# Five heads' queries and keys by seven block products, with the attention of all eight heads placed behind them

## The chip, the core and the metric

The program runs on one core of one Trainium2 chip. A core has five engines that each work through an instruction stream of their own in order: PE (TensorE, the matrix multiplies), DVE (VectorE), ACT (ScalarE), POOL (GpSimd) and SP (SyncE, which here only issues DMA transfers). They meet at semaphores. The metric is device time in microseconds of one execution, as the median of several runs; lower is better.

## The reference

One streaming step of an encoder layer: 512 prompt frames and 64 sample frames, 576 in all, each 2048 wide. What matters here is the first half of the layer, the projection and the attention:

```
hn = rmsnorm(x, g_norm1)
proj = hn @ w_in                      # 2048 x 6144: q, k, v, gb, gc, hc, 1024 columns each
q = rmsnorm(q.reshape(B, T, 8, 128), g_q);  k = rmsnorm(k.reshape(B, T, 8, 128), g_k)
z = q k^T / sqrt(128)                 # per head; mask: key before query
log_1mb = where(mask, log_sigmoid(-z), 0)
after = reverse_cumsum(log_1mb) - log_1mb
w = where(mask, exp(log_sigmoid(z) + after), 0);  o_attn = w @ v
```

The prompt attends to itself, the sample frames attend to 512 cached frames and themselves. A gated convolution over the other columns, an output projection, and a SwiGLU feed-forward layer (2048 to 5632 and back) follow; new keys and values are outputs too. Everything is float32.

## The kernel before

Activations lie feature-major: a tile is 128 features by 576 frames, cut into two halves of 288 (`HALVES`). A float32 product is made of three passes of a reduced float32 type: each operand is split into a high part and the rest (`split`: ACT copies the high part, DVE subtracts it), and PE adds high x high, low x high, high x low. One column block of 128 outputs of `w_in` takes 16 row blocks x 3 passes x 2 halves = 96 matmuls of 128x288.

**Order of work.** PE's order is written by hand, as the program records it. Side work runs as generators in a small pipeline: `pipe.tick()` is called after every three matmuls of a column (a **tick**), and `yield n` puts the rest of a generator n ticks later. SP's order is by hand too behind head 0. DVE, ACT and POOL are ordered by a scheduler, which works before the run with its own idea of how long things take. Their streams are then fixed: an instruction that waits holds all that stand behind it on its engine.

**Heads.** `head(h)` projects three column blocks, q, k and v of one head: 96 ticks. `norm_evac` normalises q and k (per frame, over 128 features): a transpose out of PSUM, squares, sums, one small matmul on PE (`ss`, L664), an inverse square root on 128x18 numbers, a scaling of 128x576, a transpose back, the gain, a split into `qh, ql` or `kh, kl`. `attend(h)` then does, each step some ticks behind the last: the scores (L730, L733) of four key blocks into three PSUM banks `z0` to `z2`; the scores of sample frames `zs`; softplus and splits of the three banks (ACT, DVE, POOL); the reverse sums as triangular matmuls (three carry groups, L780 to L783, L786 to L789, L792 to L795), after each of which `weights` caps the diagonal block (L771), takes the exponential and splits it; the product with the values `po` (L801, L804), for which `vh, vl`, the split values, are made; and `cz` and `os` for the sample frames. Between the last carry group and `po` stand 16 ticks, between `po` and `cz` 18, between `cz` and `os` 16.

**Sums of x.** The convolution columns already use block products (Strassen's scheme in Winograd's form): a unit of two column blocks by two halves of frames takes seven products of eight row blocks (24 matmuls each) and not eight. For it `conv_prepare` makes the sums of weights (DVE), their split (`whl`: ACT and DVE), and four sums of x, which `x_sums` makes during the heads: 8 pairs, 66 ticks each, through DRAM.

## Time and profile before

| | us |
|---|---|
| three runs | 2346.26, 2345.19, 2344.64 (median 2345.19) |
| profiled execution, span from first to last instruction | 2344.4 (no other time of it is given) |
| PE busy in that span | 2332.3 |
| DVE busy | 1872.3 |
| ACT busy | 1142.2 |
| POOL busy | 256.6 |

The span less the busy time of PE is 12.1 us. The granted TensorE clock is 1.000 throughout. The eight heads lie between about 32 and 435 us of the span; a period of one head is 47.2 us. A busy PE counts a matmul from its start to its modelled end (295 ns for 128x288); two that follow each other start closer than that, and the distance from start to start is what a matmul costs.

### The profile page before, as it was taken

The numbers are of one execution on the slowest core, as the hardware profiler recorded it, in microseconds if no ns is written. First come the engines' busy times: TensorE is split into PE (matmuls) and PEld (weight loads), VectorE is DVE, ScalarE is ACT, GpSimd is POOL, SyncE is SP. The second block draws the span as 40 slices with busy tenths as digits, with TensorE's granted clock in tenths as the row PEclk, the third lists the DMA queues.
The fourth block names the chain that finished last, engine by engine and source line by source line (L and its number), as shares of the span: only waits on it lengthen the run. The fifth ranks groups of instructions, "written<-read, shape, count | busy, mean of one in ns | idle before, by whom it ended". The sixth has DMA issues, their size and how long they took to land.

```text
span 2344.4 us, 43718 instructions
## 1 busy us (share of the span) xinstructions
PE 2332.3 (99%) x17573; PEld 2325.2 (99%) x17573; DVE 1872.3 (80%) x2827; ACT 1142.2 (49%) x1994; POOL 256.6 (11%) x362
## 2 busy tenths in 40 slices
PE   8999999999999999999999999999999999999999
PEld 8999999999999999999999999999999999999999
DVE  7766665788877889888888888888888777987886
ACT  6655555444445555444444444444444444444444
POOL 1111111111111220000000000000000001431121
PEclk9999999999999999999999999999999999999999
DMA  8665563774378555345345354344444936885653
GB/s 269 157 173 142 138 167 105 253 232 129 111 244 229 177 172 168 123 151 157 112 155 157 115 158 151 121 154 138 139 154 133 357 119 207 222 240 188 201 135 100
DMA packets 581762, 395.74 MB, mean 169 GB/s; under 512 B 90686, under 2 KB 570680, under 8 KB 581560
## 3 DMA queue, kind: packets, MB, share of 16 engines
q1 hardware_dynamic: 572072, 376.24, 51.7%
q0 software_dynamic: 8624, 16.22, 3.4%
q8 instruction: 137, 2.24, 0.4%
q10 hardware_dynamic: 864, 0.49, 0.1%
q14 instruction: 65, 0.53, 0.1%
HBM read 301.46 MB, written 91.44 MB: 168 GB/s over the span
## 4 chain that ended last, share of the span: by engine, by line
PE 97%; DVE 2%; DMA 1%; ACT 1%; issue 0%; SPq 0%; ACTq 0%
PE psy L1604 35%; PE psw L1604 18%; PE pj L221 15%; PE psx L1604 9%; PE psy L1094 6%; PE pjo L221 4%; PE psw L1094 3%; PE psx L1094 1%; PE pjz L221 1%; PE z L733 1%; PE po L804 1%; PE os L834 0%; PE zs L759 0%; DMA raw_a<-in_w_in_dram 0%; DMA xin<-in_x_prompt_dram 0%; DVE whl L1066 0%
## 5 line engine op out<-in xcount | busy, mean ns | idle before, releaser
L1604 PE MATMUL psy<-h_s,whl 128*128 128x288 f32 x2787 | 411.0, 294 | 0.0
L221 PE MATMUL pj<-x,whi 128*128 128x288 f32 x1856 | 388.1, 297 | 0.3 <-DVE x L375 0.3
L1604 PEld LDWEIGHTS psy<-h_s,whl 128*128 128x128 f32 x2787 | 383.3, 188 | 0.0
L231 DVE TENSOR_TENSOR whl<-raw_a,whl 128x1024 fp32r<-128x1024 f32 (+4 forms) x296 | 321.2, 1086 | 57.8 <-ACT whl L230 56.7
L1604 PE MATMUL psw<-t,whl 128*128 128x288 f32 x2400 | 347.6, 294 | 0.0
L1604 PEld LDWEIGHTS psw<-t,whl 128*128 128x128 f32 x2400 | 327.3, 188 | 0.3 <-DVE whl L231 0.2
L230 ACT CAST whl<-raw_a 128x1024 fp32r<-128x1024 f32 (+4 forms) x296 | 268.3, 907 | 101.7 <-issue 35.4
L221 PEld LDWEIGHTS pj<-x,whi 128*128 128x128 f32 x1856 | 303.5, 189 | 1.0 <-DVE x L375 0.6
L221 PE MATMUL pj<-x,wlo 128*128 128x288 f32 x928 | 274.2, 295 | 0.1
L231 DVE TENSOR_TENSOR whl<-raw_b,whl 128x1024 fp32r<-128x1024 f32 (+5 forms) x190 | 197.6, 1040 | 65.5 <-ACT whl L230 64.3
L230 ACT CAST whl<-raw_b 128x1024 fp32r<-128x1024 f32 (+5 forms) x190 | 165.4, 872 | 165.4 <-issue 72.7
L1614 ACT COPY part<-psy 128x288 f32<-128x288 f32 x242 | 96.4, 398 | 284.9 <-PE psy L1604 283.7
L1604 PE MATMUL psy<-b22m,whl 128*128 128x288 f32 x1212 | 183.1, 295 | 0.0
L1604 PE MATMUL psy<-t2t,whl 128*128 128x288 f32 x1212 | 182.8, 294 | 0.0
L221 PEld LDWEIGHTS pj<-x,wlo 128*128 128x128 f32 x928 | 174.6, 188 | 0.7 <-DVE wlo L442 0.3
L1604 PE MATMUL psx<-h_s,whl 128*128 128x288 f32 x1185 | 173.2, 294 | 0.0
L1604 PEld LDWEIGHTS psy<-t2t,whl 128*128 128x128 f32 x1212 | 168.1, 188 | 0.2 <-DVE whl L231 0.2
L1604 PEld LDWEIGHTS psy<-b22m,whl 128*128 128x128 f32 x1212 | 167.9, 188 | 0.0
L1604 PEld LDWEIGHTS psx<-h_s,whl 128*128 128x128 f32 x1185 | 162.5, 188 | 0.0
L230 ACT CAST whl<-s 128x1024 fp32r<-128x1024 f32 (+5 forms) x81 | 72.3, 892 | 101.9 <-PE psw L1604 101.9
L1383 POOL DMA_DIRECT2D hid_dram<-form x3 | 2.2, 750 | 971.1 <-DVE form L231 971.1
L1604 PE MATMUL psy<-t,whl 128*128 128x288 f32 x576 | 106.7, 295 | 0.0
(483 smaller groups left out, 4246.2 us busy)
## 6 DMA issues: line engine op xcount, KB each, us to landing
hid_dram<-form SPq DMA_DIRECT2D x147, 288.0 KB, 3.0
raw_a<-in_w_in_dram SPq DMA_DIRECT2D x41, 1024.0 KB, 6.3
raw_a<-in_w_gate_dram SPq DMA_DIRECT2D x22, 1024.0 KB, 5.8
raw_a<-in_w_up_dram SPq DMA_DIRECT2D x22, 1024.0 KB, 5.9
raw_b<-in_w_gate_dram SPq DMA_DIRECT2D x22, 1024.0 KB, 7.4
raw_b<-in_w_up_dram SPq DMA_DIRECT2D x22, 1024.0 KB, 6.6
h_s<-hid_dram SPq DMA_DIRECT2D x10, 2016.0 KB, 11.8
raw_a<-in_w_out_dram SPq DMA_DIRECT2D x16, 1024.0 KB, 5.7
```

The source lines that it names most:

```text
L221: mm(ps, w_[:, k, csl], x_, start=(k == 0 and n == 0), stop=(k == nk - 1 and n == 2))
L230: nc.scalar.copy(out=hi, in_=src)
L231: (lo_eng or nc.vector).tensor_tensor(out=lo, in0=src, in1=hi.bitcast(F32), op=ALU.subtract)
L733: mm(zb[i], a_[:, kk], b_[:, q0:TP], start=(n == 0), stop=False, skip_group_check=True)
L804: mm(po[:, i * P : 512], a_[:, i, :], b_[:, : 512 - i * P], stop=(i == 0 and n == 2), **kw)
L1094: mm(ps, whl[:, w_, j, :], x_, start=(start and j == 0 and q == 0), stop=(j == m - 1 and q == 2), skip_group_check=True)
L1383: q.dma_start(out=hid_dram[fp][2 * n - 2 : 2 * n].rearrange("f p t -> p f t"), in_=t.bitcast(F32))
L1604: mm(ps, whl[:, w_, j, :], x_, start=(start and j == 0 and q == 0), stop=(j == len(xs_) - 1 and q == 2), skip_group_check=True)
L1614: nc.scalar.copy(out=t, in_=st["y"])
```

## The change

Of the 16 blocks of queries and keys, those of heads 2 to 6 are now made by units of seven block products (`unit_prepare`, `unit_run`): columns q and k of a head by two halves of the frames, 35 products of 24 matmuls. Heads 0 and 1 (`EARLY`) come first as plain columns, in whose time `x_sums` makes the four sums of x for all 8 pairs, 12 ticks a pair, into SBUF (`xf`, `first_form`); they go to DRAM later for the convolution (`store_sums`). Then the 35 products; then, as plain columns, all values and head 7 (`LATE`, ten columns of 32 ticks). Queries and keys no longer go from PSUM into the normalisation: they are stored raw to DRAM (`put_raw`) and loaded again by `attend`, which now holds the normalisation too. `attend(h)` starts at tick 4 + 42 h of `LATE`; heads stood 96 ticks apart before. Its steps are closer: last carry group to `po` 10 ticks, `po` to `cz` 11, `cz` to `os` 11; and with heads 42 ticks apart and 101 ticks long, the normalisation of head h+1 (`ss` of q and of k) falls between the carry groups and `po` of head h. The values are loaded from DRAM shortly before `po`. Weights of `LATE` have one buffer in place of two (the other half is scratch). Counted over the whole program, PE has 120 matmuls of 128x288 fewer (16812 for 16932); ACT has 46 instructions more, DVE 36 more, SP 45 DMA issues more. Pairs of work tiles (`hl`) move to a pool of their own.

```diff
+UNIT_HEADS = (2, 3, 4, 5, 6)
+EARLY = [(0, 0), (1, 0), (0, 1), (1, 1)]
+LATE = [(2, 0), (2, 1), (2, 2), (2, 3), (2, 4), (0, 7), (1, 7), (2, 5), (2, 6), (2, 7)]
+PERIOD = 42
...
+    qk_dram = tc.dram_tile([2 * NH, P, T], F32, name="qk_dram")
...
+    for j, h in EARLY + LATE:
+        col_chunk(w_in, j * AW + h * P)
...
+    def split_later(i, end):
+        yield 8
+        if i + 1 < end:
+            split_weight(nc.vector)
+        yield 6
+        if i >= len(EARLY) and i + 2 < end:
+            load_weight()
...
+            if i == first_out - 2:
+                split_weight(nc.vector)
+            else:
+                pipe.spawn(split_later(i, end))
...
+    def load_pair_x(j, a, b):
+        x_pair[j] = [a, b]
+        for r in range(2):
+            if b is not last_x or r == 0:
+                nc.sync.dma_start(out=x_pair[j][r], in_=xt_dram[2 * j + r])
...
+            ev, od = x_pair[j]
             ge, go = g1c[:, 2 * j : 2 * j + 1], g1c[:, 2 * j + 1 : 2 * j + 2]
-            nc.scalar.activation(out=b11, in_=b11, func=AF.Copy, scale=ge)
-            nc.scalar.activation(out=b22, in_=b22, func=AF.Copy, scale=go)
-            yield 8
-            stt(out=b11, in0=b12, scalar=ge, in1=b11, op0=ALU.mult, op1=ALU.subtract)
-            yield 8
-            stt(out=b12, in0=b12, scalar=ge, in1=b22, op0=ALU.mult, op1=ALU.subtract)
-            yield 8
-            put(four[:, 0:2, :], (0, 2))
-            yield 8
-            tt(out=b22, in0=b22, in1=b11, op=ALU.subtract)
-            yield 8
-            stt(out=b21, in0=b21, scalar=go, in1=b22, op0=ALU.mult, op1=ALU.subtract)
-            yield 8
-            put(four[:, 2:4, :], (3, 1))
-            yield 8
-        free_places.append(True)
...
+            ta, tb, tc_, td = (tmp.tile([P, HALF], F32, tag=tag, name=f"x{tag}{j}") for tag in ("sq", "r", "sq", "r"))
+            nc.scalar.activation(out=ta, in_=ev[:, :HALF], func=AF.Copy, scale=ge)
+            nc.scalar.activation(out=tb, in_=od[:, HALF:], func=AF.Copy, scale=go)
+            yield 3
+            stt(out=ta, in0=ev[:, HALF:], scalar=ge, in1=ta, op0=ALU.mult, op1=ALU.subtract)
+            stt(out=tc_, in0=ev[:, HALF:], scalar=ge, in1=tb, op0=ALU.mult, op1=ALU.subtract)
+            yield 3
+            tt(out=tb, in0=tb, in1=ta, op=ALU.subtract)
+            stt(out=td, in0=od[:, :HALF], scalar=go, in1=tb, op0=ALU.mult, op1=ALU.subtract)
+            yield 2
+            split(xf[2][:, j, 0, :], xf[2][:, j, 1, :], tc_)
+            first_form[j] = slot(PLACE[j], f"xf0_{j}", F32R).rearrange("p (f t) -> p f t", f=2)
+            split(first_form[j][:, 0, :], first_form[j][:, 1, :], ta)
+            yield 2
+            split(xf[1][:, j, 0, :], xf[1][:, j, 1, :], tb)
+            split(xf[3][:, j, 0, :], xf[3][:, j, 1, :], td)
+            if j == 0:
+                load_pair_x(5, last_place(1), last_place(2))
+                load_pair_x(7, last_place(3), last_x)
+            if j in (1, 3):
+                load_pair_x(3 + j, slot(2 * j - 1, f"x{j}a"), slot(2 * j + 1, f"x{j}b"))
...
+        yield 16
+        turn("q")
+        yield 2
+        turn("k")
+        yield 4
+        qf, qh, ql = norm("q", gqs, TP)
+        yield 3
+        kb = t1.tile([P, T], F32, tag="kb", name="kb")
+        kf, kh, kl = norm("k", col("gk"), 3 * P, kb)
+        yield 2
+        nc.vector.transpose(out=cK, in_=cK)
+        yield 12
...
+        yield 3
+        put_tokens(kb, kp[:, h, :], 0, TP)
+        put_tokens(kb, ks[:, h, :], TP, T)
+        yield 14
+        vtok = t1.tile([P, 5, P], F32, tag="vtok", name="vtok")
+        nc.sync.dma_start(out=vtok[:, 0:4, :], in_=vt_dram[h, :TP].rearrange("(i p) d -> p i d", p=P))
+        nc.sync.dma_start(out=vtok[:, 4, :], in_=vt_dram[h, T - P :])
         yield 2
-        yield 8
-        kb = st["kb"]
-        if h:
-            put_tokens(kb, kp[:, h, :], 0, TP)
-            put_tokens(kb, ks[:, h, :], TP, T)
+        cV = t1.tile([P, 4, P], F32, tag="cV", name="cV")
+        nc.sync.dma_start(out=cV, in_=cv[:, h, :].rearrange("(i p) d -> p i d", p=P))
...
-        yield 18
...
         weights(2)
-        yield 5
+        yield 3
...
         weights(1)
-        yield 5
+        yield 3
...
         weights(0)
-        yield 16
-        vtok, vh, vl = st["vtok"], st["vh"], st["vl"]
+        yield 1
+        sp = scratch[:, 1280 : 1280 + T]
+        softplus(sp[:, :320], zc, sp[:, :320])
+        nc.gpsimd.tensor_tensor(out=sp[:, 256:320], in0=sp[:, 256:320], in1=s01, op=ALU.mult)
+        sh = t1.tile([P, T], F32R, tag="sph", name="sph")
+        sl = t1.tile([P, T], F32R, tag="spl", name="spl")
+        rest = sp[:, 320:]
+        nc.gpsimd.tensor_copy(rest[:, 192:256], sp[:, 256:320])
+        for b in (2, 1, 0):
+            nc.gpsimd.tensor_tensor(out=rest[:, b * TS : (b + 1) * TS], in0=rest[:, (b + 1) * TS : (b + 2) * TS],
+                                    in1=sp[:, (b + 1) * TS : (b + 2) * TS], op=ALU.add)
+        split(sh, sl, sp)
+        nc.sync.dma_start(out=vp[:, h, :].rearrange("(i p) d -> p i d", p=P), in_=vtok[:, 0:4, :])
+        nc.sync.dma_start(out=vs[:, h, :], in_=vtok[TS:, 4, :])
+        vh = t1.tile([P, 3, P], F32R, tag="vh", name="vh")
+        vl = t1.tile([P, 3, P], F32R, tag="vl", name="vl")
+        split(vh, vl, vtok[:, 0:3, :])
+        yield 9
         po = misc("po")
-        assert h < 6 or free_places
...
+        yield 11
         cz = misc("cz")
...
-        yield 16
+        yield 11
...
+    hwanted = [(0, 0, 0), (0, 0, 1), (1, 0, 0), (0, 1, 0), (0, 1, 1), (1, 0, 1), (1, 1, 0), (1, 1, 1)]
+    hwanted += [(n, c, s) for n in range(2, NHU) for c in range(2) for s in range(2)]
...
+        if first_sum:
+            tt(out=raw(1, 0), in0=raw(1, 0), in1=raw(0, 0), op=ALU.subtract)
+            if p_ == 6:
+                tt(out=own, in0=raw(1, 0), in1=raw(1, 1), op=ALU.add)
+        src = own if p_ in (3, 6) else raw(*{1: (0, 0), 2: (0, 1), 4: (1, 1), 5: (1, 0), 7: (1, 0)}[p_])
+        bt["turn"] = bt.get("turn", 0) + 1
+        whl = hoper[n, p_] = wpool.tile([P, 2, NP, P], F32R, tag=("whi", "wlo")[bt["turn"] % 2], name="whl")
+        nc.scalar.copy(out=whl[:, 0], in_=src)
+        if first_sum and p_ == 7:
+            tt(out=own, in0=raw(1, 0), in1=raw(1, 1), op=ALU.add)
+        tt(out=whl[:, 1], in0=src, in1=whl[:, 0].bitcast(F32), op=ALU.subtract)
+        gone.append(p_)
...
+        def multiply(ps, start):
+            whl = hoper.pop((n, p_))
+            for j in range(NP):
+                if p_ in (5, 6, 7, 4):
+                    q = {5: 0, 6: 1, 7: 2, 4: 3}[p_]
+                    t = xf[q][:, j] if q else first_form[j]
+                    xh, xl = t[:, 0, :], t[:, 1, :]
+                else:
+                    xh, xl = x_two(2 * j + (p_ > 1), int(p_ == 3))
+                for q, (w_, x_) in enumerate(((0, xh), (1, xh), (0, xl))):
+                    mm(ps, whl[:, w_, j, :], x_, start=(start and j == 0 and q == 0), stop=(j == NP - 1 and q == 2),
+                       skip_group_check=True)
+                pipe.tick()
...
+    def put_raw(i, ps, a, b, part=None):
+        t = tmp.tile([P, HALF], F32, tag="y", name="raw")
+        if part is None:
+            nc.scalar.copy(out=t, in_=ps)
+        else:
+            nc.vector.tensor_tensor(out=t, in0=ps, in1=part, op=ALU.add)
+        nc.sync.dma_start(out=qk_dram[i][:, a:b], in_=t)
...
+    horder = [(0, 1), (0, 2), (1, 1), (0, 7), (0, 6), (0, 5), (0, 3), (0, 4), (1, 2), (1, 6), (1, 7), (1, 5)]
+    for n in range(2, NHU):
+        if n < NHU - 1:
+            horder += [(n, 1), (n - 1, 3), (n - 1, 4), (n, 2), (n, 6), (n, 7), (n, 5)]
+        else:
+            horder += [(n, 1), (n - 1, 3), (n - 1, 4), (n, 6), (n, 7), (n, 5), (n, 2), (n, 4), (n, 3)]
...
+    def first_units():
+        yield 15
+        bt["own"] = dpool.tile([P, UC], F32, tag="uc", name="own")[:, :1024].rearrange("p (j c) -> p j c", c=P)
+        call_blocks(range(5))
...
+    for i, (j, h) in enumerate(EARLY[1:]):
+        if i == len(EARLY) - 2:
+            pipe.spawn(first_units())
+        project(raw_evac(j, h), (None, "z1") if i == 0 else (None, None))
+    for q in (2, 3):
+        unit_prepare(*horder[q])
+    pipe.flush()
+    pipe.spawn(store_sums())
+    for k_, (n, p_) in enumerate(horder):
+        unit_run(n, p_)
+        if k_ + 4 < len(horder):
+            unit_prepare(*horder[k_ + 4])
...
+        pipe.spawn(attend(h), 4 + PERIOD * h)
+    for j, h in LATE:
+        project(values_evac(h) if j == 2 else raw_evac(j, h))```

How the change stands in the streams, at three places. Names: `z_n` is a PSUM bank with scores of one head, `Eq, Ek` the queries and keys frame-major, `qf, kf` the same feature-major, `t, y, r, ms` the small numbers of the inverse square root, `whl` a split block operand, `xr` and `xf` sums of x.

**First place: DVE between the last carry group of a head and its `po`.** Before (head 4), from the cap of the second bank on:

```order
L771 SCALAR_TENSOR_TENSOR z_3130<-z_3130,acA 128x128
L178 TENSOR_TENSOR wlo_3365<-raw_a,whi_3364 128x1024
L688 TENSOR_REDUCE sums<-sq 128x9
L178 TENSOR_TENSOR wlo_3365<-raw_a,whi_3364 128x1024
L231 TENSOR_TENSOR vl<-vtok,vh 128x384
L231 TENSOR_TENSOR pl_3139<-pr_3133,ph_3136 128x384
L771 SCALAR_TENSOR_TENSOR z_3129<-z_3129,acA 128x128
L231 TENSOR_TENSOR pl_3138<-pr_3132,ph_3135 128x512
```

Now (head 1); three rows ahead of this piece stands `L823 ... z_2790`, the cap of the last bank, and the piece is the normalisation of head 2 up to its `kl`, and behind it `vl` of head 1:

```order
L738 SCALAR_TENSOR_TENSOR ms<-ss,rpad_t 128x18
L744 TENSOR_TENSOR Eq<-Eq,r 128x576
L751 STREAM_TRANSPOSE qf<-Eq 128x576
L245 TENSOR_TENSOR pl_2799<-pr_2793,ph_2796 128x512
L741 SCALAR_TENSOR_TENSOR t<-y 128x18
L742 TENSOR_TENSOR t<-t,ms 128x18
L743 SCALAR_TENSOR_TENSOR r<-t,y 128x18
L744 TENSOR_TENSOR Ek<-Ek,r 128x576
L245 TENSOR_TENSOR ql<-qf,qh 128x512
L751 STREAM_TRANSPOSE kf<-Ek 128x576
L245 TENSOR_TENSOR kl<-kf,kh 128x384
L245 TENSOR_TENSOR vl<-vtok,vh 128x384
```

The same piece of ACT's stream (head 1 with the normalisation of head 2):

```order
L244 CAST ph_2796<-pr_2793 128x512
L740 ACTIVATE y<-y 128x18
L752 ACTIVATE qf<-qf,gqs 128x576
L244 CAST qh<-qf 128x512
L752 ACTIVATE kf<-kf,vec 128x576
L244 CAST kh<-kf 128x384
L244 CAST vh<-vtok 128x384
L869 COPY o_oa<-po 128x512
```

`vl` stood beside the cap of the last bank in every head; now it stands behind the keys of the next head. On DVE there are 16, 13, 17, 4, 12, 16 and 14 instructions between the two for heads 0 to 6 (for head 7, which has no next head, none). For heads 2 and 5 they hold two evacuations and the transpose of values (`Ev`) too, for head 6 a transpose of `Ev` and one other 128x576 operation, for heads 0, 2 and 6 half a weight split (`wlo`) and for head 3 both halves, ahead of the normalisation. In head 4 `vl` stands before the transpose of the keys.

**Second place: DVE where the first products begin.** The last rows of `x_sums`, and the first operands of the units:

```order
L669 SCALAR_TENSOR_TENSOR xr_1068<-st_504,g1c,xr_1066 128x288
L245 TENSOR_TENSOR xf_585<-xr_1066,xf_585 128x288
L245 TENSOR_TENSOR xf_587<-xr_1068,xf_587 128x288
L927 TENSOR_TENSOR whl<-raw_a,whl 128x1024 x2
L918 TENSOR_TENSOR raw_a<-raw_a 128x1024
```

All 64 DVE instructions of `x_sums` stand ahead of the first `whl`. On SP the five loads of raw weights for the units stand behind the store of the third early column's second half (`L1001 DMA qk_dram<-raw`), whose copy out of PSUM stands on ACT among the copies of `x_sums` for pair 6.

**Third place: ACT where `LATE` begins.**

```order
L181 CAST whi_2163<-raw_a 128x1024 x2
L998 COPY raw<-psy 128x288
L181 CAST whi_2282<-raw_a 128x1024 x2
L728 ACTIVATE raw_a<-Eq 128x576
L728 ACTIVATE raw_a<-Ek 128x576
L739 ACTIVATE y<-ms 128x18
```

The squares of head 0 (`L728`) stand behind the split of the second late column's weights (`whi_2282`), whose load is issued when the first one's split is done.

More of the change, by code (lines that the diff above doesn't have):

```diff
@@ L452, in tile_hybrid_stream_step @@
             square(*squares.pop(0))
-        nc.sync.dma_start(out=xt_dram[KD - 1], in_=stores[0][1])
+        last_x = stores[0][1]
+        nc.sync.dma_start(out=xt_dram[KD - 1], in_=last_x)
         turn_vectors()
@@ L619, in x_sums @@
     def x_sums():
-        raw = o_half[1][:, 2:4, :]
-        four = raw.rearrange("p k (i t) -> p (k i) t", i=2)
-        b11, b12, b21, b22 = (four[:, q, :] for q in range(4))
         stt, tt = nc.vector.scalar_tensor_tensor, nc.vector.tensor_tensor
-        def put(two, names):
-            split(xs_out[:, :, 0, :], xs_out[:, :, 1, :], two)
-            for r, q in enumerate(names):
-                nc.sync.dma_start(out=xs_dram[q, j].rearrange("f p t -> p f t"), in_=xs_out[:, r].bitcast(F32))
+        yield 3
@@ L725, in attend @@
+        pl = [t1.tile([P, (512, 384, 256)[i]], F32R, tag=f"pl{i}", name=f"pl{i}") for i in range(3)]
         full = (512, 384, 384)
@@ new lines, in unit_prepare, with raw @@
+    def unit_prepare(n, p_):
+        st, tt = hst.setdefault(n, {"gone": []}), nc.vector.tensor_tensor
+        gone, own = st["gone"], bt["own"]
+        first_sum = p_ in (6, 7) and 6 not in gone and 7 not in gone
+        def raw(c, s):
+            return hregion[n, c, s][1]
+        if first_sum:
[10 more added lines that the diff above has]
+        gone.append(p_)
+        if p_ in (6, 7) and not first_sum:
+            tt(out=raw(1, 0), in0=own, in1=raw(0, 0), op=ALU.add)
+            tt(out=own, in0=raw(0, 1), in1=own, op=ALU.subtract)
+        free = {4: [(1, 1)], 5: [(1, 0)]}.get(p_, [])
+        if p_ in (2, 6, 7) and all(q in gone for q in (2, 6, 7)):
+            free = [(0, 0), (0, 1)]
+        call_blocks([hregion.pop((n, c, s))[0] for c, s in free])
@@ L978, in evac_gb @@
         def evac_gb(ps, a, b):
-            if not bt:
+            if "pool" not in bt:
                 open_b()
```

366 lines of the change are left out of this document (202 added, 164 removed).

## Prediction

> **What bounds the kernel now.** I read the page first, its busy times and the shares of the chain that ended last, then the waits of PE.
>
> ```profile
> span 2344.4 us, 43718 instructions
> PE 2332.3 (99%) x17573; PEld 2325.2 (99%) x17573; DVE 1872.3 (80%) x2827; ACT 1142.2 (49%) x1994; POOL 256.6 (11%) x362
> PE 97%; DVE 2%; DMA 1%; ACT 1%; issue 0%; SPq 0%; ACTq 0%
> ```
> ```profile
> PE psx_s L352 <- POOL acA L268: 5.0, 1, 5.0
> PE psy L1094 <- DVE whl L1066: 0.7, 1, 0.7
> ```
>
> PE is the bound from end to end. Its longest wait, 5.0 us, is at the start; nowhere else does it wait for as long as a microsecond. So a matmul that goes away is worth its whole distance to the next one, and a wait put into PE's stream costs its whole length. Next, the windows of a stage with heads and of the present block products:
>
> ```profile
> 200.00:250.00 50.00, 50.00 (x373) 49.50 (x372) 34.90 (x66) 29.63 (x59) 7.86 (x15) 1.00 0.63 177
> 550.00:600.00 50.00, 50.00 (x380) 50.00 (x379) 40.33 (x50) 21.50 (x29) 8.34 (x14) 1.00 0.38 112
> ```
>
> The columns are the window's length, then PE, PEld, DVE, ACT and POOL with counts, clock, DMA share and GB/s. Among the heads DVE has 15 us in 50 to spare and ACT 20. Block products leave DVE 10 in 50, and PE is full all the same.
>
> **What is removed: 120 matmuls.** The chain of waits gives their distance and the period of a head:
>
> ```profile
> 251.22 11.15 PE pj L221 x84
> 298.42 11.15 PE pj L221 x84
> 227.89 0.22 PE po L801 x2
> 228.11 1.58 PE po L804 x9
> 240.99 0.13 PE ss L664 x2
> ```
>
> 84 matmuls of 128x288 in 11.15 us are 0.1327 us each, so 120 are **-15.9 us**. A head's period is 298.42 - 251.22 = 47.2 us; its 288 column matmuls take 38.2, so its attention has 9.0 us of PE, which the change keeps.
>
> **What the products add.** 35 operands, each an ACT copy and a DVE subtraction of 128x1024, four sums of weights per head, evacuations, 32 stores and 16 loads of raw rows. The present products do the same per unit beside the same 168 matmuls (22.3 us), and the second window shows PE full with DVE at 40 of 50: nothing on the path. Without that cover a unit would cost DVE's 40/50 of 22.3, 18 us.
>
> **Where the products begin.** All sums of x are made in the time of three columns. Prices from the groups of instructions, the present x_sums (lines 639 to 647):
>
> ```profile
> L639 DVE SCALAR_TENSOR_TENSOR o_ob<-o_ob,g1c 128x288 f32<-128x288 f32 x8 | 5.1, 639 | 3.1 <-ACT o_ob L636 3.1
> L647 DVE SCALAR_TENSOR_TENSOR o_ob<-o_ob,g1c 128x288 f32<-128x288 f32 x8 | 4.7, 583 | 0.1
> L641 DVE SCALAR_TENSOR_TENSOR o_ob<-o_ob,g1c 128x288 f32<-128x288 f32 x8 | 4.1, 515 | 0.9 <-ACT o_ob L637 0.5
> L645 DVE TENSOR_TENSOR o_ob<-o_ob 128x288 f32<-128x288 f32 x8 | 3.6, 450 | 0.1
> L231 DVE TENSOR_TENSOR hf<-acc_a,hf 128x288 fp32r<-128x288 f32 x2 | 0.9, 458 | 2.2 <-ACT hf L230 1.9 <-DMA raw_a<-in_w_in_dram 0.2
> L178 DVE TENSOR_TENSOR wlo<-raw_a,whi 128x1024 fp32r<-128x1024 f32 x51 | 61.8, 1216 | 8.3 <-ACT whi L177 8.3
> ```
>
> Now DVE's timeline, where it is never idle:
>
> ```profile
> 267.39 1.22 DVE L178 TENSOR_TENSOR wlo<-raw_a,whi 128x1024 fp32r<-128x1024 f32 x1
> 268.52 0.55 DVE L231 TENSOR_TENSOR vl<-vtok,vh 128x384 fp32r<-128x384 f32 x1
> 268.99 0.55 DVE L231 TENSOR_TENSOR pl<-pr,ph 128x384 fp32r<-128x384 f32 x1
> ```
>
> From start to start it is 1.13 and 0.47: instructions that don't need each other overlap by 0.08 us. A pair of x costs 0.64 + 0.58 + 0.52 + 0.45 + 4 x 0.46 - 8 x 0.08 = 3.4 us, eight pairs 27; with a weight split (2.3) and two copies (0.9) some 30 us. DVE can start these near 42.5 us of the span and is done at about 73; the first product is due on PE near 71.7 us (three columns of 12.7 from 32, and 1.6 of small matmuls), and its operand takes another 1.1. I take **+2**; bounds 0 (a later due time) and 5 (the raw weights are called only after an ACT copy that stands among the sums).
>
> **Where LATE begins.** The load of the second column's weights is issued when the first products' end frees the path on SP, and head 0's squares stand behind their split.
>
> ```profile
> raw_a<-in_w_in_dram SPq DMA_DIRECT2D x41, 1024.0 KB, 6.3
> o_ob<-xt_dram SPq DMA_DIRECT2D x8, 576.0 KB, 7.0
> ```
>
> Issued at 1.3 us, landed near 8 (weights and Eq alike, 6.3 and 7.0); two ACT copies and two subtractions later, near 12, the sums of q are ready, which PE wants at tick 26, 10.4 us: 2 us. The keys, one transpose, one square and one reduction behind, cost 1 more; then the split of the third column's weights stands among the chain to the first scores: 3. I take **+6**; bounds 0 and 9.
>
> **The wait at po: the large term.** The timeline of one key normalisation, DVE and then ACT:
>
> ```profile
> 288.35 0.18 DVE L668 SCALAR_TENSOR_TENSOR ms<-ss,rpad_t 128x18 f32<-128x18 f32 x1
> 289.49 0.18 DVE L673 SCALAR_TENSOR_TENSOR r<-t,y 128x18 f32<-128x18 f32 x1
> 289.70 0.76 DVE L674 TENSOR_TENSOR Ek<-Ek,r 128x576 f32<-128x576 f32 x1
> 290.50 0.78 DVE L678 STREAM_TRANSPOSE kf<-Ek 128x576 f32<-128x576 f32 x1
> 292.66 0.56 DVE L231 TENSOR_TENSOR kl<-kf,kh 128x384 fp32r<-128x384 f32 x1 [1.39 <-ACT kh L230]
> ```
> ```profile
> 291.31 0.78 ACT L679 ACTIVATE kf<-kf,vec 128x576 f32<-128x576 f32 x1 [2.28 <-DVE kf L678]
> 292.12 0.51 ACT L230 CAST kh<-kf 128x384 fp32r<-128x384 f32 x1
> ```
>
> With nothing in its way the chain takes 4.9 us (288.35 to 293.22), with hops of 0.03 us between the engines. Before, vl did not stand behind it. Now it does, in DVE's stream, and vh in ACT's. PE's side: from the end of the last carry group to the matmul that needs vl lie 6 matmuls (0.8), ss (0.13), 24 matmuls (3.2), two passes of po (0.22) and one of its nine (0.18), **4.5 us**. More prices:
>
> ```profile
> L674 DVE TENSOR_TENSOR Eq<-Eq,r 128x576 f32<-128x576 f32 x8 | 6.2, 771 | 0.2
> L678 DVE STREAM_TRANSPOSE qf<-Eq 128x576 f32<-128x576 f32 x8 | 6.2, 776 | 0.2
> L231 DVE TENSOR_TENSOR pl<-pr,ph 128x512 fp32r<-128x512 f32 x16 | 11.0, 686 | 8.4 <-ACT ph L230 8.3
> L231 DVE TENSOR_TENSOR ql<-qf,qh 128x512 fp32r<-128x512 f32 x8 | 5.5, 692 | 9.4 <-ACT qh L230 9.4
> L230 ACT CAST vh<-vtok 128x384 fp32r<-128x384 f32 x8 | 4.1, 509 | 0.0
> L815 POOL TENSOR_TENSOR sp<-sp 128x64 f32<-128x64 f32 x24 | 10.6, 444 | 1.9
> ```
>
> DVE's side for head 1, in us after the end of that carry group. DVE reaches the cap of the bank at 1.1, held by the split of sp, which waits for POOL's sums (three of 0.44 and two shorter). Then in stream order: Eq x r 1.7 to 2.5, qf 3.3, pl 4.0, three small ones 4.5, Ek x r 5.2, ql 5.8, kf 6.5; ACT: gain 7.3, kh 7.8, vh 8.3; DVE: kl 8.4, vl **8.9**. PE wants it at 4.5 and waits 4.4 us. The other heads differ by what the streams hold: head 0 has half a weight split more but reaches the cap on time (5.1); head 2 two Ev evacuations (0.45 each), a transpose (0.78) and half a split (1.13) more (7.5); head 3 has vl ahead of the norm but behind two half splits (2.2), and its late norm then holds the scores of head 4 (2.1); head 4 has vl before kf (1.7); head 5 as head 2 without a split (6.0); head 6 two 128x576 operations and half a split more (7.5); head 7 none. The sum is **+36**. Lower bound: the chain alone, begun by ss at 0.93: 0.9 + 0.1 + 4.9 + 0.5 - 4.5 = 1.9, for heads 0, 1, 2, 5 and 6, 9.5 us. Upper: 1 us more for each of eight, 44. I take 36, since no row between is left out of the streams. POOL and SP are not late here: the values' load (3.3 us for 256 KB at its present place) is issued a dozen ticks ahead.
>
> **cz and os.** Their steps move from 18 and 16 ticks to 11 each; walked the same way, the exponential of head 1's sample weights comes 0.7 us after os is due, where a weight split stands before it: **+1.5** in all, bounds 0 and 6.
>
> **The sum:** 2344.4 - 15.9 + 2 + 6 + 36 + 1.5 = 2374. The median of the runs lies 0.8 above the span: **2375 us**. All lower bounds give 2338, all upper ones 2393.
>
> **Rivals.** (1) The streams have slack on average and the waits stay short. Per 42 ticks PE has 16.7 + 9.0 = 25.7 us; DVE's instructions for a head, its values and 1.3 splits sum to about 20.5 after overlap, ACT's to 19. If the values' split came in the gaps, the first two entries alone would remain: about 2330 to 2337. For it: a product stage at DVE 40 of 50 keeps PE full. Against: an average says nothing where one instruction stands behind a chain. (2) Only the bare chain counts (9.5 for 36, the LATE start at half): 2345, no change; the q chain and pl would have to run in its gaps. (3) PE comes back slowly after each long wait. After the 5.0 us idle at the start its first passes are slower:
>
> ```profile
> 9.16 1.97 PE L358 MATMUL psx<-ident,xin 128*128 128x128 f32 x8 [0.55 <-DMA xin<-in_x_prompt_dram]
> 13.60 0.60 PE L358 MATMUL psx<-ident,xin 128*128 128x128 f32 x4
> ```
>
> Eight take 1.97 us where later four take 0.60, so 0.8 us is lost at one return; with six to ten long waits and longer warm-ups, 2380 to 2388. [...] The profile's mean clock, 1.000, shows none of it yet.
>
> **Chances.** Forecast 0.66, rival 1 0.12, rival 2 0.08, rival 3 0.14. What can be told from no change here is about 0.2%, 4.7 us: faster 0.12, same 0.08, slower 0.80. The range **2342 to 2392** leaves out rival 1 and a little above; the forecast's own is 2358 to 2390.
>
> **What would show it.** PE waits at po on vl or vh, 4 to 8 us in heads 0, 1, 2, 5, 6; at ss and the scores of head 0; 2 us at the first product. The products' own windows full, the convolution and all behind it unchanged but for the shift. Wrong if PE is full in the LATE windows, or waits there for a DMA instead.

## The result, and the profile after

The changed kernel takes **2399.22 us** (median, 2398.41 to 2399.75), the kernel before 2344.99 us beside it: a ratio of **1.0229, 95% interval 1.0215 to 1.0244**. It is slower, as forecast, but by 54 us and not by 30: the time lies 7 us above the range. Page of the changed kernel (busy times, shares of the chain):

```profile
span 2397.5 us, 43680 instructions
PE 2338.8 (98%) x17453; PEld 2324.9 (97%) x17453; DVE 1908.4 (80%) x2863; ACT 1168.6 (49%) x2040; POOL 258.0 (11%) x362
PE 80%; DVE 10%; ACT 3%; DMA 3%; issue 2%; POOL 1%; SPq 1%; DVEq 0%; ACTq 0%; POOLq 0%
```

PE has 120 matmuls fewer (17453 for 17573), and yet 6.5 us more busy time: some of them ran slower. Of the chain that ended last PE had 97% and has 80%. The first convolution product tells where the time came from (matmuls of that line: count, duration min/median/max, first and last start), before and after:

```profile
L1094 PE MATMUL psy<-x,whl x624: 292/294/398, 475.1 to 676.1; 128*128 128x288 f32 x156
```
```profile
L1271 PE MATMUL psy<-x,whl x624: 290/294/399, 527.2 to 728.6; 128*128 128x288 f32 x156
```

It starts 52.1 us later, of 53.1 in all: nearly everything happens ahead of the convolution. Before, the only wait of PE over a microsecond was one of 5.0 us at the start. Now its waits over the whole span are (in all, times, longest):

```profile
PE po L868 <- ACT vh L244: 26.8, 7, 6.1
PE po L868 <- DVE vl L245: 7.8, 6, 1.9
PE ps_eps L491 <- DVE spread L486: 5.2, 1, 5.2
PE psx_s L373 <- POOL acA L287: 4.6, 1, 4.6
PE ss L734 <- DVE raw_a L729: 3.1, 1, 3.1
PE z L783 <- ACT kh L244: 1.7, 2, 1.2
PE z L783 <- DVE kl L245: 1.2, 2, 0.9
PE os L886 <- issue: 0.8, 1, 0.8
```

34.6 us stand at po, behind vh and vl; 6.8 at ss, the scores and os; 5.2 at a small matmul named ps_eps. The windows show the second loss (window, length, then PE, PEld, DVE, ACT, POOL, granted clock, DMA share, GB/s), one of the block products and three of the heads:

```profile
100.00:150.00 50.00, 50.00 (x380) 50.00 (x380) 32.01 (x33) 18.88 (x24) 0.00 (x0) 1.00 0.72 232
200.00:250.00 50.00, 40.13 (x257) 37.99 (x256) 34.71 (x67) 27.16 (x56) 6.95 (x14) 0.90 0.49 129
300.00:350.00 50.00, 39.56 (x260) 37.56 (x260) 31.36 (x64) 29.51 (x63) 10.22 (x19) 0.90 0.42 111
400.00:450.00 50.00, 37.70 (x244) 35.79 (x244) 29.99 (x60) 27.98 (x58) 10.51 (x17) 0.86 0.42 101
```

The products keep PE full, with DVE at 32 of 50. Among the heads PE stands still for 10 to 12 us in 50, and the granted clock is 0.86 to 0.90 where it was 1.00 before. Around the wait of head 1:

```profile
269.50 0.38 PE L865 MATMUL po<-pr,vtok 128*128 128x128 f32 x2
275.21 0.58 PE L868 MATMUL po<-ph,vh 128*128 128x256 f32 x1 [5.32 <-ACT vh L244]
```
```profile
273.00:274.00 1.00, 0.00 (x0) 0.00 (x0) 0.39 (x1) 0.58 (x1) 0.77 (x1) 0.99 0.00 0
274.00:275.00 1.00, 0.00 (x0) 0.00 (x0) 0.23 (x1) 0.97 (x3) 0.00 (x0) 0.50 0.19 62
279.00:280.00 1.00, 1.00 (x6) 1.00 (x6) 0.00 (x0) 0.96 (x2) 0.00 (x0) 0.50 0.00 0
280.00:281.00 1.00, 1.00 (x7) 1.00 (x6) 0.00 (x0) 0.00 (x0) 0.80 (x1) 0.60 0.00 0
281.00:282.00 1.00, 1.00 (x9) 1.00 (x9) 0.00 (x0) 0.00 (x0) 0.00 (x0) 1.00 0.00 0
```

PE stops at 269.9. The clock falls to 0.50 at 274.0, and it stays there until 280.8, more than five microseconds after the wait is over: the window at 279 holds 6 matmuls and the one at 281 holds 9, and a matmul of 128x288 starts 0.24 us after the last one in place of 0.13.

**Where the 52.1 us come from**, by the start-to-start distance of every PE matmul up to that convolution product: 120 matmuls fewer, -15.9; PE's idle time, 47.8 for 1.6 (as these records have it), +46.2; half clock while PE works, +15.7 (3.0 behind ps_eps, 12.7 among the heads); and a rest of +6.3. Of the rest 4.9 stand at the edges of the waits, where no next matmul overlaps the last one (some 0.25 us for each of two dozen waits); the other 1.4 are not placed. The sum is 52.3.

### The profile page after: what moved, and what is told of

It is laid out like the page before. It is cut to its first block, busy times and chain, and to the rows that moved or that the text cites. A ratio compares the mean times of both kernels' runs of the same rounds, so it can differ in the third digit from the quotient of the medians.

```text
span 2397.5 us, 43680 instructions
## 1 busy us (share of the span) xinstructions
PE 2338.8 (98%) x17453; PEld 2324.9 (97%) x17453; DVE 1908.4 (80%) x2863; ACT 1168.6 (49%) x2040; POOL 258.0 (11%) x362
## 4 chain that ended last, share of the span: by engine, by line
PE 80%; DVE 10%; ACT 3%; DMA 3%; issue 2%; POOL 1%; SPq 1%; DVEq 0%; ACTq 0%; POOLq 0%
PE psy L1783 33%; PE psw L1783 17%; PE psx L1783 8%; PE psy L1271 5%; PE pj L235 4%; PE psw L1271 3%; PE psy L950 3%; PE psw L950 1%; PE psx L1271 1%; DVE wlo L182 1%; PE po L868 1%; DMA raw_a<-in_w_out_dram 1%; PE psx L950 1%; DMA form_dram<-hf 1%; SPq L1980 1%
## 5 line engine op out<-in xcount | busy, mean ns | idle before, releaser
L245 DVE TENSOR_TENSOR whl<-raw_a,whl 128x1024 fp32r<-128x1024 f32 (+4 forms) x296 | 318.1, 1075 | 59.1 <-ACT whl L244 58.2
L244 ACT CAST whl<-raw_a 128x1024 fp32r<-128x1024 f32 (+4 forms) x296 | 267.9, 906 | 104.9 <-issue 35.4
L235 PE MATMUL pj<-x,whi 128*128 128x288 f32 x1248 | 275.2, 304 | 0.6 <-DVE x L396 0.3
L245 DVE TENSOR_TENSOR whl<-raw_b,whl 128x1024 fp32r<-128x1024 f32 (+5 forms) x190 | 196.7, 1035 | 66.5 <-ACT whl L244 65.3
L244 ACT CAST whl<-raw_b 128x1024 fp32r<-128x1024 f32 (+5 forms) x190 | 165.5, 872 | 168.4 <-issue 72.9
L235 PEld LDWEIGHTS pj<-x,whi 128*128 128x128 f32 x1248 | 212.1, 194 | 2.2 <-DVE x L396 1.3
L235 PE MATMUL pj<-x,wlo 128*128 128x288 f32 x624 | 187.7, 301 | 0.1
L235 PEld LDWEIGHTS pj<-x,wlo 128*128 128x128 f32 x624 | 120.9, 194 | 0.9 <-DVE wlo L463 0.3
L244 ACT CAST whl<-s 128x1024 fp32r<-128x1024 f32 (+5 forms) x81 | 72.3, 893 | 100.4 <-PE psw L1783 100.3
```

What stands on the lines that cost most here:

```text
L235: mm(ps, w_[:, k, csl], x_, start=(k == 0 and n == 0), stop=(k == nk - 1 and n == 2))
L244: nc.scalar.copy(out=hi, in_=src)
L245: (lo_eng or nc.vector).tensor_tensor(out=lo, in0=src, in1=hi.bitcast(F32), op=ALU.subtract)
```

## The experiments

The theory after the result (A): PE waits because instructions that it needs stand behind others in the fixed order of DVE and ACT, and each longer wait is paid a second time at half clock. The rivals: (B) DVE and ACT have no time left with a head each 42 ticks, so that a repair only moves the waits; (C) half clock comes with this stage, not with the waits. The ratio is to the kernel before on the same chip (its medians were 2345.0 to 2346.2), with its 95% interval.

| run | median us | ratio |
|---|---|---|
| the change | 2399.2 | 1.0229 (1.0215 to 1.0244) |
| fill_po | 2392.8 | 1.0201 (1.0184 to 1.0218) |
| values_first | 2387.5 | 1.0177 (1.0161 to 1.0192) |
| eps_later | 2394.4 | 1.0204 (1.0189 to 1.0219) |
| three_edits | 2378.5 | 1.0137 (1.0122 to 1.0153) |
| norm_early | 2396.6 | 1.0220 (1.0204 to 1.0235) |
| all_edits_41 | 2375.6 | 1.0130 (1.0113 to 1.0147) |
| all_edits_42 | 2385.3 | 1.0170 (1.0154 to 1.0185) |
| hand_order | 2376.7 | 1.0132 (1.0115 to 1.0149) |
| hand_order_all | 2370.2 | 1.0109 (1.0094 to 1.0124) |
| hand_order_46 | 2391.5 | 1.0197 (1.0182 to 1.0212) |
| bare_chain | 2356.4 | 1.0053 (1.0036 to 1.0069) |
| bare_chain_3 | 2352.4 | 1.0029 (1.0018 to 1.0041) |
| bare_chain_5 | 2354.4 | 1.0035 (1.0023 to 1.0048) |
| bare_chain_43 | 2349.6 | 1.0014 (1.0005 to 1.0023) |
| front_43 | 2348.3 | 1.0010 (1.0001 to 1.0019) |
| front_44 | 2353.6 | 1.0035 (1.0021 to 1.0048) |

### Is half clock a consequence of the waits? (fill_po)

```diff
         po = misc("po")
+        for _ in range(26 if h in (0, 1, 2, 5, 6) else 0):
+            mm(po[:, :HALF], trir, x_two(0, 0)[0], start=True, stop=True, skip_group_check=True)
```

> The change with 26 extra matmuls of 128x288 put ahead of po in heads 0, 1, 2, 5 and 6, into the bank of po, whose first real matmul starts over (the result is the same). At 0.133 us each they take 3.45 us inside waits that were 3.9 to 6.8 us long. Theory A (a long idle wait of PE is what sets its clock to half, for whole stretches of 3.41 us): the time that PE stands still falls below 3.4 us at each of the five, the clock stays at 1.00 there, and the work lost at half clock behind them (2.7 + 2.8 + 3.1 + 2.3 + 1.8 = 12.6 us) comes back: about 2387 us. Theory C (the half clock comes with this stage and not from the waits): stretches of half clock stay, about 2399 us.

Its waits at po, and two of its windows, behind the wait of head 1 and that of head 2:

```profile
PE po L870 <- ACT vh L244: 9.3, 7, 2.6
PE po L870 <- DVE vl L245: 8.8, 7, 2.0
```
```profile
271.00:272.00 1.00, 1.00 (x7) 0.87 (x6) 0.00 (x0) 0.00 (x0) 0.00 (x0) 1.00 0.00 0
...
301.00:302.00 1.00, 0.05 (x1) 0.05 (x1) 0.97 (x4) 1.00 (x3) 0.00 (x0) 1.00 0.00 0
...
306.00:307.00 1.00, 1.00 (x4) 0.81 (x3) 0.00 (x0) 0.00 (x0) 0.00 (x0) 0.50 0.77 88
```

The waits shrink by 16.5 us, about the 17 us of the filling. In head 1, whose wait is now 1.2 and 0.3 us, the clock stays at 1.00, so C falls: more work on PE, and the half clock of that head is gone, as it is in head 0. All stretches at half clock ahead of the convolution sum to 47.8 us in the change and to 27.3 here (mean clock 0.990 and 0.994). But only half of the 12.6 us came back, and the median lies between what A and C gave. Heads 3 and 4, whose waits (1.9 and 2.6 us) were not filled, have a stretch of 3.4 us each here and had none in the change. In head 2 PE now waits 2.3 us, does one matmul and waits 2.0 us, and the clock halves all the same, for 3.4 us where it was 10.2 before. The limit of 3.4 us for one wait, on which my number rested, was a guess that no trace showed, and it is wrong: two waits of 2.3 and 2.0 us were enough here, and one of 3.1 us in the change (see the last section).

### What do the values cost at po? (values_first)

```diff
+        pins[h + 1] = (nc.scalar.copy(out=vh, in_=vtok[:, 0:3, :]).ins,
+                       nc.vector.tensor_tensor(out=vl, in0=vtok[:, 0:3, :], in1=vh.bitcast(F32), op=ALU.subtract).ins)
         yield 3
...
-        split(vh, vl, vtok[:, 0:3, :])
...
-        qf, qh, ql = norm("q", gqs, TP)
+        with behind(h):
+            qf, qh, ql = norm("q", gqs, TP)
```

`behind(h)` queues what is written inside it behind the two instructions, on their engines; keys alike.

> The change, with the split of the values (vh, vl) written ahead of the normalisation of the next head, whose instructions on DVE and ACT are queued behind it; nothing else is edited. Theory A (the waits at po come from vl and vh standing behind the next head's keys): the 34.6 us of waits at po fall below 5, the half clock in heads 0, 1, 2, 5 and 6 goes (12.6 us), the scores of the next head wait some 1 us each because the normalisation now ends later: 2399 - 34.6 - 12.6 + 7 = 2359 us, 2350 to 2367. Theory B (DVE and ACT have no slack left with a head each 42 ticks): the waits come back at the scores, cz and os in the same sum, 2385 to 2400 us.

Its waits:

```profile
PE z L793 <- ACT kh L244: 11.7, 6, 2.7
PE po L876 <- ACT whi L181: 4.3, 3, 1.9
PE po L876 <- issue: 4.1, 2, 2.6
PE z L793 <- DVE kl L245: 2.6, 6, 1.2
```

The 34.6 us at po fall to 8.4, and 14.3 us come up at the scores, twice what I allowed. The values were not the cause alone. Put first, they hold the normalisation, and with it the next head's scores. The waits among the heads are shorter (2.7 at most), but eight stretches at half clock stand among them, 41.0 us with the one behind ps_eps (mean clock 0.991). 12 us came back of 40, and 2387.5 lies in the range of B.

### ps_eps and the start (eps_later, three_edits)

```diff
-    pipe.spawn(row_eps(), 4)
-    pipe.spawn(row_scale(), 10)
+    pipe.spawn(row_eps(), 23)
+    pipe.spawn(row_scale(), 29)
```

> The change, with the one small matmul ps_eps (and the one for the row scale) at ticks 23 and 29 as in the kernel before, instead of 4 and 10. Theory A: the 5.2 us wait for DVE's sums of squares and the 6.8 us at half clock behind it (3.1 us lost) go, so PE comes 8.3 us sooner to the first product; DVE's sums of x are not sooner, and 2 to 3 us of wait appear there: about 2393 us. Rival: all of it comes back as a wait at the first product, 2398 to 2399. Without any wait there 2391.

The wait of 5.2 us is gone, and all that the trace has between the start and the first late column is this:

```profile
PE ps_r1s L501 <- DVE rpad_t L492: 1.0, 1, 1.0
```

No wait came up at the first product: PE arrived 7 us sooner (its first product starts at 73.2 us of the span in place of 80.1) and its operand was there, so the 2 us of the prediction, and the 2 to 3 of this expectation, were not. The median fell by 4.8, not 8.3: besides this 1.0, two heads fell into one more stretch of half clock than in the change (mean clock 0.990 in both).

three_edits joins both edits and begins head 0 later:

```diff
-        pipe.spawn(attend(h), 4 + PERIOD * h)
+        pipe.spawn(attend(h), 12 + PERIOD * h)
```

> The values first and ps_eps later as in the two other runs, and head 0 begun at tick 12 and not 4 of the last ten columns (each head 8 ticks later), so that the load of its raw queries has landed. Theory A: 2359 - 6 for ps_eps - 6 for the waits at the first ss and the first scores - 1.7 for half clock behind them = 2345 us, 2337 to 2353. Theory B: 2380 or more.

2378.5 us, far above the range of A and 1.5 below the bound of B. The wait at ss is gone, 19.4 us stand at the scores and 11.8 at po. Ahead of the convolution PE stands still for as long as in values_first (34.5 and 34.8 us); what fell is the half clock, from 41.0 us to 17.1 (mean clock 0.991 and 0.996).

### Another place for the normalisation (norm_early, all_edits_41, all_edits_42)

```diff
         nc.vector.transpose(out=cK, in_=cK)
-        yield 12
+        yield 24
```

> The change, with 12 more ticks between the normalisation of a head and its scores (every step behind it 12 ticks later, the loads of cached keys 11 ticks behind those of the queries), so that the normalisation of head h+1 no longer falls between the carry groups and po of head h, but ahead of the carry groups. Theory A2 (what made PE wait is that values, normalisation and the next scores all fall into the 7 us behind the last carry group; DVE and ACT have time enough elsewhere): waits at po and at the scores under 1 us each, 8 in all, no half clock behind them: 2399 - 37 + 8 - 12.6 - 2 = 2355 us, 2346 to 2364. Theory B (DVE and ACT have no slack with a head each 42 ticks): the waits come back elsewhere, at the carry groups, cz or os; 2380 or more.

> The normalisation early as in norm_early, ps_eps at tick 23 as in eps_later, head 0 begun at tick 10, heads 41 ticks apart, po to cz and cz to os 9 ticks each. Theory A2: 2355 - 5 for ps_eps - 8 for the start of the last ten columns and the half clock behind it, + 3 for the closer steps = 2345 us, 2335 to 2352. Theory B: 2370 or more.

> As all_edits_41, with heads 42 ticks apart and head 0 begun at tick 8; the last head's final step is then forced 7 ticks early. Theory A2: within 3 us of all_edits_41. Theory B: below all_edits_41 by 7 or more, since 41 ticks are the tighter.

The median of norm_early is 2.6 us below that of the change, but its runs lie between 2393.1 and 2401.3, on both sides of it, so no gain is shown. Its waits:

```profile
PE po L869 <- ACT vh L244: 12.7, 7, 2.7
PE ss L730 <- DVE raw_a L725: 12.2, 7, 3.6
PE po L869 <- DVE vl L245: 10.0, 7, 2.5
```

The waits moved again, to ss (the sums of squares are late now) and, though the normalisation was out of the way, to po. In DVE's order vl stood behind two evacuations and the transpose of other values and half a weight split:

```profile
277.59 0.81 DVE L1017 TENSOR_TENSOR Ev<-pj,R 128x288 f32<-128x288 f32 x2
278.43 0.78 DVE L1012 STREAM_TRANSPOSE Ev<-Ev 128x576 f32<-128x576 f32 x1
279.14 1.18 DVE L182 TENSOR_TENSOR wlo<-raw_a,whi 128x1024 fp32r<-128x1024 f32 x1
280.24 0.55 DVE L245 TENSOR_TENSOR vl<-vtok,vh 128x384 fp32r<-128x384 f32 x1
```

That looks like B, and 2396.6 and 2375.6 (all_edits_41) keep to its bounds. But with all edits heads 41 ticks apart beat 42 by 10 us, against B: the tighter of two is the faster. PE waits 5.4 us less there ahead of the convolution (28.6 for 34.0), and has 17.1 us at half clock in place of 34.1 (mean clock 0.996 and 0.993). The scheduler's order differs between the two; that this is the reason is not shown. So I set the order itself.

### The order by hand (hand_order, hand_order_all, hand_order_46)

```diff
-        weights(0)
+        with behind(h + 1):
+            last = weights(0)
...
+        with tc.issue_after(last[0]), tc.issue_after(last[1]):
             split(sh, sl, sp)
...
+        with behind(("k", h + 1)):
             nc.scalar.copy(out=o_attn[h][:, :TP], in_=po)
```

beside the pins of values_first, the values loaded 12 ticks sooner, and those of head 5 projected two columns sooner.

> The change at the same ticks, with the order of DVE and ACT behind the last carry group set by hand for five instructions: the values loaded at tick 44 (the last block, for the sample frames, apart at 56; the values of head 5 projected two columns sooner, so that they are in time), vh and vl ahead of the last cap, the next head's normalisation behind vl but ahead of the split of the last bank, the split of sp behind that, and the copy of po behind kh. Theory A3 (waits come from what stands in the order of two streams, not from their load): po waits under 3 us in all, the scores 0 to 1 us each because the normalisation ends 8.4 us behind the carry group and the scores are due at 8.7, no half clock but at the start: 2399 - 37 + 5 - 12.6 - 3 = 2351 us, 2342 to 2362. Theory B (the streams have no slack with a head each 42 ticks, whatever the order): 2375 or more.

> hand_order with ps_eps at tick 23 and head 0 begun at tick 12. Theory A3: 2351 - 5 - 8 = 2338 us, 2330 to 2350, faster than the kernel before. Theory B: 2362 or more.

> hand_order_all with heads 46 ticks apart and head 0 begun at tick 8; the last 19 ticks of head 7 are then run without cover, 3 to 5 us. Theory A3: no waits left to take away, so 2 to 5 us more than hand_order_all. Theory B: each head has 1.6 us more of PE to hide in, 7 heads, so 5 to 10 us less than hand_order_all in spite of the end.

hand_order has 1.5 us of waits left at po (34.6 in the change) and 17.3 at the scores. hand_order_46 gives each head 1.6 us more of PE, and it is **slower** by 21 us: its order put the sums late, and PE waits 13.7 us at ss (head 0 also begins at tick 8 in place of 12). More room did not help and a worse order hurt, which is against B, although the bounds that B gave for hand_order and hand_order_all (2375 and 2362 or more) held, and 21 us more is not what A gave either. What was left in hand_order_all is seen in the chain of waits, from vl to the scores of one head (start, length, what):

```profile
283.46 0.44 DVE vl L859
...
286.45 0.77 DVE qf L759
287.22 0.64 DVE spl L245
287.85 1.14 DVE wlo L182
288.99 0.60 DVE ql L762
289.59 0.09 DVE t L749
289.68 1.22 DVE wlo L182
...
291.23 0.77 DVE Ek L752
...
293.64 0.52 ACT kh L761
```

spl and two halves of a weight split, 3.0 us, stand between the queries and the keys. PE waited 3.2 us for these keys.

### The chain laid bare (bare_chain and its variants)

```diff
-        split(sh, sl, sp)
...
+        with behind(("kl", h + 1)):
+            split(sh, sl, sp)
         po = misc("po")
```

and the halves of a weight split that would fall inside the chain are queued behind the transpose kf, or begun up to 12 ticks later.

> hand_order_all with two more things taken out of the chain from the last carry group to the next head's scores: the split of sp goes behind kl, and the halves of a weight split (wlo) that fell between Eq and kl go behind the transpose kf (or are begun up to 12 ticks later). Theory A4 (the waits that are left are the other DVE work inside that chain, 0.64 + 2.35 us in the heads where it was seen): the waits at the scores, 19 us in hand_order_all, fall below 6, and the half clock (17 us at half, 8.5 lost) goes: 2370 - 13 - 8 - 2 = 2347 us, 2340 to 2356. Theory B (no slack): the waits move to cz, os or to the weights of a column; 2362 or more.

> bare_chain with 3 more ticks between the normalisation and the scores (1.2 us more for the chain, and every later step of a head 3 ticks later), head 0 begun at tick 10. Theory A4: the chain from vl to kl is 6.8 us of which none waits for PE, so 1.2 us more of time takes what is left of the waits at the scores: 2 to 6 us below bare_chain, 2338 to 2350. Theory B: no better than bare_chain.

14 us for these edits, and 4 more for 3 ticks (with the split of the values a step sooner and head 0 at tick 10): the waits at the scores were 19.0 us in hand_order_all and are 11.3 and 9.1, the mean clock of the profiled executions 0.998 and 0.999. The direction is the one that A gives, its sizes (2347, and 2338 to 2350) were too good by 9 and 2 us. With heads still 42 ticks apart, PE's idle time ahead of the convolution is 12.0 us in bare_chain_3 where it was 47.8 in the change, and DVE is busy for 42 us in 50 between 200 and 250 us of the span: the waits went without more time, which B doesn't allow for. Four more runs took what was left:

> bare_chain_3 with 2 more ticks between the normalisation and the scores (5 in all), the values' split ahead of the first carry group, both halves of a weight split behind kf wherever a normalisation was written up to 22 ticks before, and ps_eps and the row scale 11 and 17 ticks later (34 and 46). Theory A4: of the 9.1 us of waits at the scores and 3.4 us lost at half clock in bare_chain_3, 2 us of waits stay and no half clock, the 1.0 us at the row scale goes: 2352 - 7 - 3 - 1 = 2341 us, 2336 to 2346, faster than the kernel before by 1 to 9. Theory B (the streams have no slack): 2350 or more, with new waits at po, cz or os.

> bare_chain_5 with heads 43 ticks apart; 17 ticks of the last head then run without cover (2 to 3 us). Theory A4: the same time as bare_chain_5 plus 1 to 3 us. Theory B: each head has 0.4 us more, and it is faster.

> bare_chain_43 with the squares and sums of the queries and keys 2 ticks further ahead of ss, 1 more tick between the normalisation and the scores and 1 between cz and os, and the second half of a weight split behind kl (the first stays behind kf). Theory A4: of bare_chain_43's waits (2.6 at ss, 4.7 at the scores, 3.2 at os, with 3.8 lost at half clock) half goes: 2349.5 - 5 - 2 = 2342 us, 2338 to 2347. Theory B: no better than bare_chain_43.

> front_43 with heads 44 ticks apart and one tick more between the normalisation and the scores; 26 ticks of the last head run without cover. Theory A4: 1 to 4 us more than front_43, for the uncovered end. Theory B: faster than front_43.

bare_chain_5 is no better than bare_chain_3, as B had it. One tick more for each head (43) is worth 4.8 us, as B had it. A second one (44, beside front_43) costs 5.3, the way A had it, if by more than its 1 to 4. front_43 itself is 1.3 us below bare_chain_43, with runs that overlap, and not the 7 that A gave. In front_43, which has the lowest median, with the sums two ticks sooner and the second half of each weight split behind kl, waits and clock are:

```profile
PE os L923 <- issue: 3.4, 3, 1.8
PE pj L249 <- DVE wlo L182: 2.9, 3, 1.4
PE ss L756 <- DVE raw_a L751: 1.6, 4, 0.6
PE z L812 <- ACT kh L775: 0.5, 1, 0.5
```
```profile
200.00:250.00 50.00, 48.13 (x351) 46.45 (x350) 41.33 (x80) 36.70 (x75) 9.66 (x21) 1.00 0.55 132
300.00:350.00 50.00, 49.02 (x357) 47.60 (x356) 42.40 (x82) 38.93 (x86) 14.83 (x28) 1.00 0.54 138
```

PE is busy for 48 to 49 us of 50 at full clock, and DVE for 41 to 42. The median of front_43 is 2.8 us above the kernel before; the interval, 1.0001 to 1.0019, lies just above 1. In the profiled execution (2346.4 us, without half clock) PE has gained 1.7 us up to the first convolution product; idle time of 9.8 us, in waits of under 2 us each, at os, the columns, the first products, ss and the scores, eats most of the rest of the 15.9. No version beat the kernel before.

## Why the prediction was wrong

**Right:** slower, and why. The 120 matmuls are worth 15.9 us by their distance; the products hide all their work; PE waits at po for vl and vh behind the next head's keys. Head by head in us, as walked and as the trace has it:

| | h0 | h1 | h2 | h3 | h4 | h5 | h6 | h7 |
|---|---|---|---|---|---|---|---|---|
| walked | 5.1 | 4.4 | 7.5 | 2.2 | 1.7 | 6.0 | 7.5 | 0 |
| measured | 5.2 | 5.3 | 7.1 | 1.9 | 2.6 | 5.5 | 6.8 | 0 |

In sum 34.4 walked (36.5 with 2.1 for the scores of head 4; the prediction put down 36), and 34.6 measured, with 1.4 at the scores of head 4. For the chain of head 1 the walk had vl at 8.9 us behind the carry group's end, and the trace has 10.4. The start of the late columns was put at 6: 3.1 at ss and 1.5 at the first scores came. cz and os: 1.5, measured 0.8. Waits in all 45.5, measured 46.2. That these two agree is partly luck: 5.2 us of the second stand at a place that was not forecast, and make up for what came smaller elsewhere.

**Wrong, first and largest: the waits were priced at their length.** The step that failed is that a wait in PE's stream "costs its whole length": it costs more, and rival 3 should have been part of the sum. Rival 3 took 0.8 us for one return, from the transposes at the start, and a chance of 0.14, because the mean clock before was 1.000. But the kernel before has one long wait, at its start, where there was no full-speed work to lose, and its mean clock could not show that start: the trace's record of the clock begins at 11.2 us of the span. Ahead of that a transposing pass of 128x128 starts 0.213 us after the last one, and from 12.5 us on 0.109 us, so PE went at about half pace there. Measured in the changed kernel: 15.7 us lost at half clock, in seven stretches that hold or follow a wait of 3 to 7 us, 2.2 each; and 6.3 us more, most of it lost overlap at the edges of two dozen waits, which no term held. With the 22 us the forecast's own waits give 2397. Rival 3's longer warm-ups, with which it gave 2380 to 2388, were a guess that no trace of before shows; the change's trace has 3.4 to 10.2 us at half clock in each of the seven, a part of it inside the wait.

**Wrong, second: ps_eps was missed.** 5.2 us of wait, and 3.0 lost at half clock behind it. The two spawns stand at ticks 4 and 10 where they stood at 23 and 29, and the prediction began its walk only at the sums of x. After:

```profile
38.95 0.61 PE L491 MATMUL ps_eps<-spread,acA 128*128 128x18 f32 x2 [5.20 <-DVE spread L486]
```
```profile
40.00:50.00 10.00, 10.00 (x58) 9.81 (x58) 9.62 (x24) 5.82 (x14) 0.00 (x0) 0.74 1.01 351
```

DVE and ACT square x there until 38 us in either kernel; the matmul was moved ahead of their end. In that window PE does 58 matmuls where it did 77.

**Wrong, third, and small: the first product.** 2 us, measured 0, in eps_later too, where PE comes 7 us sooner.

**What the cause was not.** That vl stands behind the keys is how PE came to wait, but not the cause by itself: with vl first PE waited for the keys (values_first). The cause is the whole of DVE's and ACT's work between the last carry group and the next scores, in an order made without regard to it; setting that order by hand brought 43 of the 54 us back at the same 42 ticks (bare_chain; ps_eps later and the later start are in it, worth 6.5 between hand_order and hand_order_all, and some weight splits are begun later). As forecasts the times of A were no good: every run for which A gave a range came out above it (bare_chain by 0.4 us), and the bounds of B held in seven. What speaks for A is not these times, but that PE's waits went from 47.8 to 12.0 us while each head kept its 42 ticks. Whether the last few us are a matter of order or of time is open: 43 ticks beat 42 by 4.8 us, which speaks for time; 44 lost to 43 and 46 to 42, which speaks for order.

## What to carry to other kernels

Price a wait on PE at more than its length: here 46.2 us of waits brought another 22 us with them, and the profile before never showed it. When steps are packed more closely, walk the whole stretch between two uses of PE on each in-order engine and not the one late instruction: repairing that one hands the wait to the next. And look for small matmuls that a rewrite moves ahead of their operands; two numbers in a spawn cost 5 to 7 us here (4.8 in the median of eps_later, 7.0 at its first product).

## What the runs showed of the hardware

In the profiled execution of the change the granted clock is 0.50 in these stretches ahead of the convolution, with the waits of PE that end just before them or in them (us of the span, by the modelled ends of the matmuls):

| half clock from | for | waits of PE: start, length |
|---|---|---|
| 38.46 | 6.83 | 33.75, 5.20 |
| 205.71 | 3.41 | 201.67, 3.10 |
| 239.84 | 6.83 | 236.14, 4.46; 241.18, 0.74 |
| 273.98 | 6.83 | 269.89, 5.32 |
| 308.11 | 10.24 | 305.01, 5.36; 310.95, 1.77 |
| 403.68 | 6.83 | 400.46, 3.92; 404.96, 1.58 |
| 437.81 | 6.83 | 434.20, 6.06; 440.85, 0.73 |

The lengths are one, two or three times 3.41 us, and from start to start it is 49, 10, 10, 10, 28 and 10 times as much (34.13 us for 10). Half clock began 3.1 to 4.7 us after PE had stopped, in one case (205.71) 0.9 us after the wait was over. From 15 us of the span up to the convolution, the longest wait in the same execution that none followed is one of 1.94 us, 0.4 us behind one of 0.71 (head 4).

A single long wait was not needed: in head 2 of fill_po PE waits 2.3 us, does one matmul of 0.39 us and waits 2.0 us, and the clock is at half for 3.4 us from 303.7 on. Nor does the length of the waits settle what they cost: eps_later has those of the change at po (34.8 us for 34.6, the longest 6.1 in both) and none at ps_eps, and yet the same mean clock, 0.990. What made the difference is not shown. The four runs of values_first lie between 2383.3 and 2392.0 us, with a mean clock of 0.994 in the lowest and 0.991 in the highest; the reason for that is not shown either.
